# Differential attention with the two maps subtracted undivided, and the first map's sum folded into the head norm

## The chip, the cores and the metric

The kernel runs on one core of a Trainium2 chip. The metric is the device time of one execution in microseconds, as a median over runs. The core has five engines that matter here: TensorE (PE in the profile, with its weight loads as PEld), VectorE (DVE), ScalarE (ACT), GpSimd (POOL) and SyncE (SP), which issues most DMAs. Each engine works through its own queue in order, and they wait for each other by semaphores. In the views used below, times are microseconds from the start of the span unless marked ns, and L497 means line 497 of the kernel.

## The reference

The program is a decoder trunk of two layers over 512 tokens of width 1024. Each layer has a mixer (differential attention, a short convolution and a gated linear attention, whose outputs are concatenated and projected) and then a layer of 16384 single-neuron experts. The change touches the differential attention only:

```python
s = jnp.einsum('bqhmd,bkhmd->bhmqk', qi, k).astype(jnp.float32) * scale
p = jax.nn.softmax(jnp.where(mask, s, -jnp.inf), axis=-1)
a = p[:, :, 0] - lam * p[:, :, 1]
return jnp.einsum('bhqk,bkhe->bqhe', a.astype(v.dtype), v)
...
o = rmsnorm(o, gain) * out_scale
```

There are four heads, each with two maps (m = 0 and 1) of 64-wide queries and keys, and with values 128 wide. Each map has its own softmax. The second map is weighted with `lam`, one number per layer, and subtracted from the first; the difference is multiplied with the values. The result of each head is then normalised over its 128 columns (`rmsnorm`: divided by the root of the mean of its squares plus 1e-6). `lam` is exp(sum of lam_q1 * lam_k1) - exp(sum of lam_q2 * lam_k2) + lam_init.

## The kernel before, in words

The kernel runs the two layers one after the other, each as a mixer and an expert stage. The expert stages take most of the span and aren't touched. The mixer holds tokens in four blocks of 128 (`tb`). It projects the normalised input with slabs of 256 columns of the input weights; each product is three f32r matmuls of split operands (`mm3`, L79 to L81). `across` and `down` are generators that yield one projected tile (`psp`) at a time.

Attention runs for one block of queries at a time, in `diff_attention`, for tb = 0 to 3, with tb + 1 blocks of keys (128, 256, 384 or 512 columns). For each of the four heads:

- `head_weights` makes, for each map, one score product into PSUM (`pss`, L486), adds the causal mask by a second product (L487), and takes the row maximum (L488). The exponential (L493) reads PSUM, writes the map into the tile `e`, and gives the row's sum through its accumulator output, into a column of the small tile `st`. Then VectorE takes the reciprocal of both sums (L495), multiplies the second by `lam` (L496), scales the second map by it (L497), and scales the first map and subtracts the second in one instruction (L498).
- `diff_attention` transposes the difference on TensorE (`atr`, L512), copies it to SBUF (`aT`, L514, ScalarE), and multiplies it with the values into one quarter of the PSUM tile `po` (L516).

When all four heads of a block are in `po`, `head_norm` squares the whole tile (L524, ScalarE, 512 columns), sums the squares per head (L525, VectorE), makes the reciprocal root with a few small VectorE steps (`rsqrt`, L173 to L188) and scales `po` by it into `ho` (L527). `head_out` transposes that (`htr`, L535) and splits it for the output projection (`mh`, `ml`, L536 and L537).

The first two blocks are computed between the projections for the convolution (L375 to L382). The first two heads of block 2 are computed early, inside the last such projection (L393 to L396), and given to `diff_attention` as `early`. Blocks 2 and 3 run beside the loading and splitting of the output weights (`woraw` to `woh` and `wol`, L409 and L410) and beside the output projection (`pso`, L426), whose products with the other mixers' outputs don't need the attention.

The order of the instructions in each queue isn't that of the program text. A planner orders them from the data they need, the buffers that are free, the order in the text and the estimated cost of each, unless the text pins them (`keep_in_program_order`); nothing around this change in the mixer is pinned. So projection matmuls stand between those of the attention in TensorE's queue. PSUM holds four buffers for score tiles (`psA`), two for `po`, `atr` and `htr` (`psB`) and two for projections (`psC`). The small tiles `st` rotate through four buffers.

Of the kernel before, what the change touches and what calls it, by code (L numbers as in the profile page):

```python
# [7 lines left out]
F32 = mybir.dt.float32  # L8
# [5 lines left out]
AF = mybir.ActivationFunctionType  # L14
OP = mybir.AluOpType
AX = mybir.AxisListType
# [3 lines left out]
P = 128  # L20
# [43 lines left out]
def bc(ap, pattern):  # L64
    return bass.AP(tensor=ap.tensor, offset=ap.offset, ap=[ap.ap[0]] + pattern)


class K:
# [152 lines left out]
    def mixer(self, L):  # L221
        nc, tc, ins = self.nc, self.tc, self.ins
        lam_init = 0.8 - 0.6 * math.exp(-0.3 * L)
        right = ExitStack()
        with ExitStack() as mc:
# [4 lines left out]
            kT = mp.tile([P, 4, T], F32, name="kT")  # L230
# [7 lines left out]
            with ExitStack() as wc:  # L238
# [29 lines left out]
                def across(c0, n=256):  # L268
                    wh, wl = slab(c0, n)
                    for j in range(n // P):  # L270
                        ps = self.psC.tile([P, T], F32, tag="c", name="psp")
                        for k in range(KD):
                            self.mm3(ps, wh[:, k, j * P:j * P + P], wl[:, k, j * P:j * P + P], hh[:, k], hl[:, k],
                                     k == 0, k == KD - 1)
                        yield j, ps
# [34 lines left out]
                for i in range(2):  # L310
                    nc.vector.scalar_tensor_tensor(lt, lamv[:, 2 * i], 1.0, lamv[:, 2 * i + 1], op0=OP.mult,
                                                   op1=OP.mult, accum_out=ld[:, i:i + 1])
                le = mp.tile([P, 2], F32, name="le")
                nc.scalar.activation(le, ld, AF.Exp)
                lam = mp.tile([P, 1], F32, name="lam")
                nc.vector.tensor_tensor(lam, le[:, 0:1], le[:, 1:2], op=OP.subtract)
                nc.vector.tensor_scalar(lam, lam, lam_init, None, op0=OP.add)
                nc.vector.tensor_scalar(dgain, dgain, 1.0 - lam_init, None, op0=OP.mult)
                wh, wl = slab(2816, 272)
                for tb in range(TB):  # L320
# [25 lines left out]
                for i in range(4):  # L346
                    dst, h = (qT, kT)[i // 2], i % 2
# [18 lines left out]
                ap = ac.enter_context(tc.tile_pool(name="attn", bufs=2, side="right", reuse_waits="tile"))  # L366
                qz = [ap.tile([P, 4, 2, P], F32, name=f"qz{i}", bufs=1) for i in range(2)]
# [18 lines left out]
                for j in range(2):  # L386
                    y = yt[:, j]
                    nc.vector.tensor_scalar(y, z[:, j, 0:T], cw[:, j, 0:1], None, op0=OP.mult)
                    for w in (1, 2):
                        nc.vector.scalar_tensor_tensor(y, z[:, j, w:w + T], cw[:, j, w:w + 1], y,  # L390
                                                       op0=OP.mult, op1=OP.add)
                    ys.append(y)
                for j, ps in across(1536):  # L393
                    if j == 0:
                        self.turned_queries(2, qT, qz[0])
                        early = [self.head_weights(2, h, kT, qz[0], lam, ap) for h in range(2)]  # L396
                    nc.vector.tensor_tensor(ys[j], ys[j], ps, op=OP.mult)
                    self.split(mch[:, j], mcl[:, j], ys[j])

# [76 lines left out]
            r = slice(64 * m, 64 * m + 64)  # L476
            self.nc.scalar.copy(qz[r, :, m], qT[r, :, s])

    def head_weights(self, tb, h, kT, qz, lam, ap):
        nc = self.nc  # L480
        nk = (tb + 1) * P
        st = self.sm.tile([P, 8], F32, tag="st", name="st")
        pss = []
        for m in range(2):
            ps = self.psA.tile([P, T], F32, tag="a", name="pss")
            nc.tensor.matmul(ps[:, 0:nk], qz[:, h, m], kT[:, h, 0:nk], start=True, stop=False)  # L486
            nc.tensor.matmul(ps[:, tb * P:nk], self.identb, self.causal, start=False, stop=True)  # L487
            nc.vector.tensor_reduce(st[:, m:m + 1], ps[:, 0:nk], axis=AX.X, op=OP.max)  # L488
            pss.append(ps)
        nc.vector.tensor_scalar(st[:, 2:4], st[:, 0:2], -0.125, None, op0=OP.mult)  # L490
        e = ap.tile([P, 2, T], F32, tag="e", name="e")
        for m in range(2):
            nc.scalar.activation(e[:, m, 0:nk], pss[m][:, 0:nk], AF.Exp, bias=st[:, 2 + m:3 + m],  # L493
                                 scale=0.125, accum_out=st[:, 4 + m:5 + m])
        nc.vector.reciprocal(st[:, 6:8], st[:, 4:6])  # L495
        nc.vector.tensor_tensor(st[:, 7:8], st[:, 7:8], lam, op=OP.mult)  # L496
        nc.vector.tensor_scalar(e[:, 1, 0:nk], e[:, 1, 0:nk], st[:, 7:8], None, op0=OP.mult)  # L497
        nc.vector.scalar_tensor_tensor(e[:, 0, 0:nk], e[:, 0, 0:nk], st[:, 6:7], e[:, 1, 0:nk],  # L498
                                       op0=OP.mult, op1=OP.subtract)
        return e  # L500

    def diff_attention(self, tb, qT, kT, va, qz, lam, ap, early=()):
        nc = self.nc
        early = list(early)
        if not early:
            self.turned_queries(tb, qT, qz)
        po = self.psB.tile([P, 4, P], F32, tag="b", name="po")
        for h in range(4):
            e = early.pop(0) if early else self.head_weights(tb, h, kT, qz, lam, ap)
            tr = self.psB.tile([P, 4, P], F32, tag="b", name="atr")  # L510
            for kb in range(tb + 1):
                nc.tensor.transpose(tr[:, kb], e[:, 0, kb * P:kb * P + P], self.ident)  # L512
            aT = ap.tile([P, 4, P], F32, tag="aT", name="aT")
            nc.scalar.copy(aT[:, 0:tb + 1], tr[:, 0:tb + 1])  # L514
            for kb in range(tb + 1):
                nc.tensor.matmul(po[:, h], aT[:, kb], va[:, kb, h * P:h * P + P],  # L516
                                 start=(kb == 0), stop=(kb == tb))
        return self.head_norm(po, 4, P, ap)

    def head_norm(self, po, nh, hd, pool):  # L520
        nc = self.nc
        o = pool.tile([P, nh, hd], F32, tag="ho", name="ho", bufs=2)
        ss = self.sm.tile([P, nh], F32, tag="hss", name="hss")
        nc.scalar.activation(o, po, AF.Square)  # L524
        nc.vector.tensor_reduce(ss, o, axis=AX.X, op=OP.add)  # L525
        rstd = self.rsqrt(ss, hd)
        nc.vector.tensor_tensor(o, po, bc(rstd, [[1, nh], [0, hd]]), op=OP.mult)  # L527
        return o.rearrange("p h d -> p (h d)")

# [752 lines left out]
```

## Time and profile before

| what | us |
|---|---|
| median of 3 runs | 2959.73 |
| the runs | 2958.84 to 2962.85 |
| the profiled execution, its own time | 2958.37 |
| span of the profiled execution, first to last instruction | 2956.6 |

The granted TensorE clock was 0.999 of full speed. The profile gives busy time per engine, the same per stretch of the span, the idle time of an engine together with what released it, groups of instructions by line and shape, and the chain of work that ended last, followed backwards through the releasers. The matmuls are pipelined and their ends are modelled, so a busy TensorE isn't one at its peak. The lines that matter are shown in the prediction, where they are used.

### The profile page before, as it was taken

How to read it: one execution, taken by the hardware profiler on the slowest of the kernel's cores; microseconds unless marked ns; L12 is line 12 of the kernel's file. 1: busy time of each engine (PE TensorE's matmuls, PEld its weight loads, DVE VectorE, ACT ScalarE, POOL GpSimd, SP SyncE). 2: the span in 40 equal slices, each digit the busy share in tenths (PEclk: the TensorE clock that was granted, in tenths of full speed). 3: DMA queues.
4: the chain of work that ended last, by engine and by line, in shares of the span. 5: the costliest groups of instructions: out<-in, count | busy, mean ns of one | idle time of the engine just before them, and what ended most of it. 6: DMA issues, size and time to landing. Idle time of an engine off the chain costs nothing.

```text
span 2956.6 us, 44538 instructions
## 1 busy us (share of the span) xinstructions
PE 2925.6 (99%) x16262; PEld 2606.0 (88%) x16262; DVE 2394.7 (81%) x4754; ACT 1256.3 (42%) x1860; POOL 716.0 (24%) x617
## 2 busy tenths in 40 slices
PE   8999999999999999999999999999999999999998
PEld 7878899999999999888888788999999999988887
DVE  6676999976887788877866769999768787888778
ACT  6253355665333332333453433556653333333333
POOL 1200000222444455222012000012225444452220
PEclk9999999999999999999999999999999999999999
DMA  4322257999999998999633222679999999989995
GB/s 130 92 72 77 93 172 250 321 301 362 348 338 326 330 346 310 368 333 342 251 96 90 67 82 86 205 253 330 303 351 356 333 337 332 332 316 358 346 347 203
DMA packets 335835, 760.24 MB, mean 257 GB/s; under 512 B 30688, under 2 KB 191360, under 8 KB 331520
## 3 DMA queue, kind: packets, MB, share of 16 engines
q1 hardware_dynamic: 160624, 435.19, 41.4%
q0 software_dynamic: 75776, 271.62, 26.0%
q10 hardware_dynamic: 99216, 50.60, 5.7%
q8 instruction: 127, 2.08, 0.3%
q14 instruction: 92, 0.75, 0.1%
HBM read 673.15 MB, written 81.00 MB: 255 GB/s over the span
## 4 chain that ended last, share of the span: by engine, by line
PE 84%; DVE 11%; ACT 2%; issue 2%; DMA 1%; SPq 0%; DVEq 0%; ACTq 0%
PE pv L80 11%; PE pv L81 11%; PE pv L79 11%; PE psh L79 9%; PE psh L81 9%; PE psh L80 9%; PE psp L80 2%; PE psp L81 2%; PE psp L79 2%; PE psq L80 2%; PE psq L79 2%; PE psq L81 2%; PE pss L486 1%; PE psg L1211 1%; PE pss L764 1%
## 5 line engine op out<-in xcount | busy, mean ns | idle before, releaser
L827 POOL DMA_INDIRECT row<-in_u_rows,idx x256 | 349.1, 1363 | 1337.6 <-DVE row L834 627.8
L80 PE MATMUL pv<-vl,wh 128*128 128x512 f32 x1500 | 583.9, 389 | 0.4 <-DVE vl L931 0.3
L81 PE MATMUL pv<-vh,wl 128*128 128x512 f32 x1500 | 583.4, 389 | 0.0
L79 PE MATMUL pv<-vh,wh 128*128 128x512 f32 x1500 | 583.2, 389 | 0.0
L827 POOL DMA_INDIRECT row<-in_v_rows,idx x256 | 315.7, 1233 | 597.0 <-DVE yacc L843 548.2
L745 ACT ACTIVATE ht<-psh 128x384 f32<-128x384 f32 x256 | 125.7, 491 | 742.1 <-PE psh L81 741.9
L931 DVE TENSOR_TENSOR vl<-vraw,vh 128x1024 fp32r<-128x1024 f32 x250 | 305.9, 1224 | 115.2 <-ACT vh L936 104.2
L79 PE MATMUL psh<-ahi,uwb 128*128 128x384 f32 x1024 | 346.9, 339 | 0.0
L79 PE MATMUL psh<-ahi,uwa 128*128 128x384 f32 x1024 | 346.4, 338 | 0.0
L81 PE MATMUL psh<-ahi,uwa 128*128 128x384 f32 x1024 | 344.6, 337 | 0.7 <-DVE uwa L730 0.7
L80 PE MATMUL psh<-alo,uwa 128*128 128x384 f32 x1024 | 344.3, 336 | 0.0
L80 PE MATMUL psh<-alo,uwb 128*128 128x384 f32 x1024 | 344.2, 336 | 0.0
L81 PE MATMUL psh<-ahi,uwb 128*128 128x384 f32 x1024 | 344.1, 336 | 0.0
L81 PEld LDWEIGHTS pv<-vh,wl 128*128 128x128 f32 x1500 | 281.4, 188 | 59.6 <-DVE wl L931 1.0
L80 PEld LDWEIGHTS pv<-vl,wh 128*128 128x128 f32 x1500 | 281.4, 188 | 56.6 <-DVE vl L931 2.2
L79 PEld LDWEIGHTS pv<-vh,wh 128*128 128x128 f32 x1500 | 281.6, 188 | 53.9
L843 DVE SCALAR_TENSOR_TENSOR yacc<-row,wk,yacc 128x1024 f32<-128x1024 f32 x254 | 325.2, 1280 | 1.7
L944 ACT CAST wh<-ht 128x384 fp32r<-128x384 f32 x250 | 127.9, 512 | 433.6 <-DVE ht L1096 417.0
L834 DVE SCALAR_TENSOR_TENSOR row<-row,xg 128x1024 f32<-128x1024 f32 x256 | 308.0, 1219 | 0.0
L730 DVE TENSOR_TENSOR uwa<-uraw,uwa 128x1024 fp32r<-128x1024 f32 x144 | 175.7, 1223 | 134.7 <-ACT uwa L729 134.5
L936 ACT CAST vh<-vraw 128x1024 fp32r<-128x1024 f32 x250 | 262.6, 1050 | 9.7 <-DMA vraw<-in_v_rows 9.7
L730 DVE TENSOR_TENSOR uwb<-uraw,uwb 128x1024 fp32r<-128x1024 f32 x144 | 175.8, 1222 | 105.9 <-ACT uwb L729 105.9
(361 smaller groups left out, 5708.6 us busy)
## 6 DMA issues: line engine op xcount, KB each, us to landing
uraw<-in_peer_u SPq DMA_DIRECT2D x256, 512.0 KB, 5.6
vraw<-in_v_rows SPq DMA_DIRECT2D x256, 512.0 KB, 6.5
G<-stg ACTq DMA_DIRECT2D x48, 1024.0 KB, 7.6
g<-G SPq DMA_DIRECT2D x32, 1536.0 KB, 10.0
H<-ht SPq DMA_DIRECT2D x144, 192.0 KB, 4.7
ht<-H SPq DMA_DIRECT2D x144, 192.0 KB, 6.5
wraw<-in_w_in SPq DMA_DIRECT2D x84, 256.0 KB, 3.2
uraw<-in_peer_w_q SPq DMA_DIRECT2D x32, 512.0 KB, 3.5
```

The lines of the kernel that those rows point to most:

```text
L79: mm(ps, ah, bh, start=first, stop=False)
L80: mm(ps, ah, bl, start=False, stop=False)
L81: mm(ps, al, bh, start=False, stop=last)
L486: nc.tensor.matmul(ps[:, 0:nk], qz[:, h, m], kT[:, h, 0:nk], start=True, stop=False)
L730: self.last = pin(nc.vector.tensor_tensor(lo, src, hi.bitcast(F32), op=OP.subtract))
L745: pin(nc.scalar.activation(hs[c], ps, AF.Gelu))
L827: nc.gpsimd.indirect_dma_start(out=r, out_offset=None, in_=ins[name], in_offset=bass.IndirectOffsetOnAxis(ap=idx[:, k:k + 1], axis=0))
L834: nc.vector.scalar_tensor_tensor(r, r, 1.0, xg, op0=OP.mult, op1=OP.mult, accum_out=hd[:, k:k + 1])
L843: nc.vector.scalar_tensor_tensor(yacc, r, wk[:, k:k + 1], yacc, op0=OP.mult, op1=OP.add)
L931: self.last = pin(nc.vector.tensor_tensor(lo, src, hi.bitcast(F32), op=OP.subtract))
L936: pin(nc.scalar.copy(vh[c], vs[c]))
L944: pin(nc.scalar.copy(wh[c], hs[c]))
```

## The change

The division of each map by its sum is rewritten. With sums s0 and s1 of the exponentials e0 and e1, the difference e0/s0 - lam * e1/s1 is 1/s0 times (e0 - lam * s0/s1 * e1). The kernel now forms the bracket, with one VectorE instruction over the map, and multiplies it with the values undivided. The factor 1/s0 belongs to a row and a head, so it is applied behind the product: the four sums s0 of a block are collected in a tile `s0` of four columns, `head_norm` takes their reciprocal, passes it as scale to a Square per head (with the sum of squares through its accumulator output, in place of the reduce), and multiplies it into the norm's factor. `lam` is computed with its sign turned, so that the subtraction becomes an addition.

```diff
-                nc.vector.tensor_tensor(lam, le[:, 0:1], le[:, 1:2], op=OP.subtract)
-                nc.vector.tensor_scalar(lam, lam, lam_init, None, op0=OP.add)
+                nc.vector.tensor_tensor(lam, le[:, 1:2], le[:, 0:1], op=OP.subtract)
+                nc.vector.tensor_scalar(lam, lam, lam_init, None, op0=OP.subtract)
...
-                        early = [self.head_weights(2, h, kT, qz[0], lam, ap) for h in range(2)]
+                        s0 = self.sums()
+                        early = [s0] + [self.head_weights(2, h, kT, qz[0], lam, ap, s0) for h in range(2)]
...
-    def head_weights(self, tb, h, kT, qz, lam, ap):
+    def head_weights(self, tb, h, kT, qz, lam, ap, s0):
...
-        st = self.sm.tile([P, 8], F32, tag="st", name="st")
+        st = self.sm.tile([P, 6], F32, tag="st", name="st")
...
             nc.scalar.activation(e[:, m, 0:nk], pss[m][:, 0:nk], AF.Exp, bias=st[:, 2 + m:3 + m],
-                                 scale=0.125, accum_out=st[:, 4 + m:5 + m])
-        nc.vector.reciprocal(st[:, 6:8], st[:, 4:6])
-        nc.vector.tensor_tensor(st[:, 7:8], st[:, 7:8], lam, op=OP.mult)
-        nc.vector.tensor_scalar(e[:, 1, 0:nk], e[:, 1, 0:nk], st[:, 7:8], None, op0=OP.mult)
-        nc.vector.scalar_tensor_tensor(e[:, 0, 0:nk], e[:, 0, 0:nk], st[:, 6:7], e[:, 1, 0:nk],
-                                       op0=OP.mult, op1=OP.subtract)
+                                 scale=0.125, accum_out=st[:, 4:5] if m else s0[:, h:h + 1])
+        nc.vector.reciprocal(st[:, 4:5], st[:, 4:5])
+        nc.vector.scalar_tensor_tensor(st[:, 5:6], st[:, 4:5], lam, s0[:, h:h + 1], op0=OP.mult, op1=OP.mult)
+        nc.vector.scalar_tensor_tensor(e[:, 0, 0:nk], e[:, 1, 0:nk], st[:, 5:6], e[:, 0, 0:nk],
+                                       op0=OP.mult, op1=OP.add)
...
             self.turned_queries(tb, qT, qz)
+            s0 = self.sums()
+        else:
+            s0 = early.pop(0)
...
-        return self.head_norm(po, 4, P, ap)
-
-    def head_norm(self, po, nh, hd, pool):
+        return self.head_norm(po, 4, P, ap, s0)
+
+    def sums(self):
+        return self.sm.tile([P, 4], F32, tag="s0", name="s0")
+
+    def head_norm(self, po, nh, hd, pool, s0):
...
-        nc.scalar.activation(o, po, AF.Square)
-        nc.vector.tensor_reduce(ss, o, axis=AX.X, op=OP.add)
+        nc.vector.reciprocal(s0, s0)
+        for h in range(nh):
+            nc.scalar.activation(o[:, h], po[:, h], AF.Square, scale=s0[:, h:h + 1], accum_out=ss[:, h:h + 1])
         rstd = self.rsqrt(ss, hd)
+        nc.vector.tensor_tensor(rstd, rstd, s0, op=OP.mult)
         nc.vector.tensor_tensor(o, po, bc(rstd, [[1, nh], [0, hd]]), op=OP.mult)
```

More of the change, by code (lines that the diff above doesn't have):

```diff
@@ L506, in diff_attention @@
             self.turned_queries(tb, qT, qz)
+            s0 = self.sums()
+        else:
+            s0 = early.pop(0)
         po = self.psB.tile([P, 4, P], F32, tag="b", name="po")
         for h in range(4):
-            e = early.pop(0) if early else self.head_weights(tb, h, kT, qz, lam, ap)
+            e = early.pop(0) if early else self.head_weights(tb, h, kT, qz, lam, ap, s0)
             tr = self.psB.tile([P, 4, P], F32, tag="b", name="atr")
```

## The prediction

> **What bounds the kernel now.** I read the page first, its busy times and its chain, to learn which engine sets the end.
>
> ```profile
> PE 2925.6 (99%) x16262; PEld 2606.0 (88%) x16262; DVE 2394.7 (81%) x4754; ACT 1256.3 (42%) x1860; POOL 716.0 (24%) x617
> PE 84%; DVE 11%; ACT 2%; issue 2%; DMA 1%; SPq 0%; DVEq 0%; ACTq 0%
> ```
>
> TensorE is busy 99% of the span. The chain lies on VectorE for 11%, though, so I asked for the stretches in which the changed lines run: attention in layer 0 (150 to 250 us), attention in layer 1 (about 1619 to 1719 us), and for comparison the projections before them. The columns are the stretch, its length, then busy time with the instruction count of PE, PEld (weight loads), DVE, ACT and POOL, the granted clock, DMA share and GB/s.
>
> ```profile
> 100.00:150.00 50.00, 50.00 (x343) 46.28 (x342) 28.62 (x47) 14.83 (x27) 13.14 (x23) 1.00 0.33 85
> 150.00:200.00 50.00, 49.86 (x248) 37.35 (x247) 36.12 (x114) 23.56 (x69) 0.00 (x0) 1.00 0.15 48
> 200.00:250.00 50.00, 48.93 (x251) 35.99 (x250) 39.49 (x96) 25.58 (x51) 0.00 (x0) 1.00 0.31 106
> 1669.00:1719.00 50.00, 48.53 (x249) 36.53 (x250) 38.83 (x95) 26.15 (x52) 0.00 (x0) 1.00 0.32 106
> 1670.00:1690.00 20.00, 19.77 (x92) 13.20 (x91) 19.02 (x46) 12.95 (x25) 0.00 (x0) 1.00 0.50 155
> ```
>
> PE is busy there too, since the order of the work puts projection matmuls between the attention's own. VectorE is nearly full only in 1670 to 1690 us (19.02 of 20). Busy PE need not be PE at its peak, so I went to the waits, of the matmuls over the whole run, then of the weight loads in the two attentions (total us, times, longest):
>
> ```profile
> PE po L516 <- ACT aT L514: 1.2, 2, 0.6
> ...
> PE pso L79 <- ACT woh L84: 0.9, 2, 0.6
> ```
> ```profile
> PEld po L516 <- ACT aT L514: 5.4, 16, 0.9
> ...
> PEld atr L512 <- issue: 1.1, 4, 0.4
> ...
> PEld htr L535 <- DVE ho L527: 0.5, 1, 0.5
> PEld pso L80 <- DVE wol L85: 0.4, 2, 0.2
> ...
> PEld pso L80 <- DVE st L490: 0.3, 1, 0.3
> ```
> ```profile
> PEld po L516 <- ACT aT L514: 5.0, 15, 0.9
> PEld pso L79 <- ACT woh L84: 1.7, 2, 1.1
> ...
> PEld htr L535 <- DVE ho L527: 0.5, 1, 0.5
> ```
>
> The result of the edited head chain is `e`, written at L498 and read by the transposes `atr` at L512. No row names L498 as releaser: the transposes wait 1.1 us in all, for their own issue. So the instruction which the change brings forward has nobody waiting for it.
>
> **The change part by part.** These are the groups by line, shapes kept apart (busy us, mean ns):
>
> ```profile
> L525 DVE TENSOR_REDUCE hss<-ho 128x4 f32<-128x512 f32 x8 | 5.5, 684 | 12.5 <-ACT ho L524 12.5
> L495 DVE RECIPROCAL st<-st 128x2 f32<-128x2 f32 x32 | 5.2, 163 | 7.3 <-ACT e L493 7.3
> L496 DVE TENSOR_TENSOR st<-st,lam 128x1 f32<-128x1 f32 x32 | 5.0, 157 | 0.7
> ...
> L497 DVE TENSOR_SCALAR e<-e,st 128x512 f32<-128x512 f32 x8 | 3.9, 483 | 0.3
> L497 DVE TENSOR_SCALAR e<-e,st 128x384 f32<-128x384 f32 x8 | 3.3, 418 | 0.4
> L185 DVE SCALAR_TENSOR_TENSOR rt<-rt 128x1 f32<-128x1 f32 x20 | 3.2, 159 | 0.6
> L497 DVE TENSOR_SCALAR e<-e,st 128x256 f32<-128x256 f32 x8 | 2.8, 350 | 0.4
> ...
> L497 DVE TENSOR_SCALAR e<-e,st 128x128 f32<-128x128 f32 x8 | 2.3, 282 | 0.4
> ```
>
> *Each of 32 heads.* The scaling of the second map (L497) goes: 8 x (0.282 + 0.350 + 0.418 + 0.483) = 12.3 us of VectorE. The reciprocal stays, one column instead of two. The one-column multiply by lam (0.157) becomes a one-column scalar_tensor_tensor, for which L185 is the nearest row (0.159): nothing. The subtraction L498 keeps its form and sizes. Writing the first map's sum into another tile costs nothing, and the two lines for lam only swap operands.
>
> *Each of 8 blocks.* The reduce goes: 8 x 0.684 = 5.5 us. A reciprocal and a multiply on four columns come in: 8 x (0.163 + 0.157) = 2.6 us. VectorE is left 12.3 + 5.5 - 2.6 = 15.2 us lighter. One Square of 512 columns becomes four of 128, each with an accumulator read. The trace has no such Square; the nearest rows are the exponentials of 128 columns, which have a pointer operand and an accumulator too (start, us), and beside them the last block's end in layer 0:
>
> ```profile
> 153.10 0.36 ACT L493 ACTIVATE e<-pss,st 128x128 f32<-128x128 f32 x1
> ...
> 154.14 0.37 ACT L493 ACTIVATE e<-pss,st 128x128 f32<-128x128 f32 x1
> 154.39 0.21 ACT L493 ACTIVATION_READ_ACCUMULATOR e<-pss,st 128x1 f32 x1
> ```
> ```profile
> 233.91 0.60 ACT L524 ACTIVATE ho<-po 128x512 f32<-128x512 f32 x1 [1.25 <-PE po L516]
> 238.56 0.69 ACT L536 ACTIVATE mh<-htr,dgain 128x512 fp32r<-128x512 f32 x1 [4.05 <-PE htr L535]
> ```
> ```profile
> 235.26 0.17 DVE L173 TENSOR_SCALAR rv<-hss 128x4 f32<-128x4 f32 x1
> 235.46 0.17 DVE L175 TENSOR_SCALAR ry<-rv 128x4 int32<-128x4 int32 x1
> ```
>
> Four such exponentials in a row take from 153.10 to 154.39 + 0.21 = 154.60: 1.50 us. In the place of the Square's 0.60, ScalarE gets 0.90 more per block, 7.2 us in all, and has room for it on the whole (42%). From Square to the first step of the norm it was 235.26 - 233.91 = 1.35 us and becomes 1.50: 0.15 longer. The extra multiply adds one step of the small operations, 235.46 - 235.26 = 0.20. The reciprocal of the sums needs only the last head's exponential and the sums' last reader, so it is done while that head is transposed and multiplied. Each block's end is 0.35 us longer. This is taken from the exponentials, since they do the same work in form; the other end is four Squares as cheap as the one, 0.60, with one read behind it (154.39 + 0.21 - 154.14 - 0.37 = 0.09): then the end would be 1.35 - 0.69 - 0.20 = 0.46 shorter.
>
> [...]
>
> *What lies on the path.* First, the end of block 3, once per layer: `htr` waits for `ho` (0.5 us in both lists), so 0.35 more is exposed, 0.7 in all. Output projection matmuls that don't need this block stand right behind, and the order written for the longer chain can put one of them ahead: I take half, +0.4; without that cover it is 0.7, and with cheap Squares the waits of 0.5 go.
>
> Second, the output weights. In layer 1 their split (L84, L85) shares VectorE's full stretch, 1670 to 1690 us, with four of the L497, whose row for that stretch is
>
> ```profile
> 1670.00:1690.00 20.00, 1.79 (x4) 1.00 0.50 155
> ```
>
> and with block 2's reduce: 1.79 + 0.68 = 2.5 us go, and 0.3 come back. Raw buffers come free sooner by up to that much, so the last load is issued sooner, and the 0.9 us for which PE waited for `woh` can go: -0.9. The bounds are nothing, and all that weight loads waited for `woh`, `ho` (twice), `wol` and `st`: 1.7 + 0.5 + 0.5 + 0.4 + 0.3 = 3.4 us. What is late next is PE itself, which has no long wait here besides that for `aT`.
>
> Third, the other heads and the ends of blocks 0 to 2: 0, since nobody waits for L498, and no wait of `htr` is listed but the one. The waits for `aT` (L514) are those of transpose, copy and product in turn, which the change leaves alone. No DMA, no matmul, no POOL instruction is added or moved past another.
>
> The sum: 0.4 - 0.9 + 0 = -0.5 us. Made against the profiled execution it is 2958.37 - 0.5 = 2957.9 us (span 2956.6 and 1.8 around it). The median of the three runs lies 1.36 us above that execution, so the median to expect is 2959.73 - 0.5 = 2959.2 us. A measurement of this kernel tells about 0.2% from no change, 5.9 us; the forecast is no difference.
>
> **The rivals.** *The head chain paces attention.* If PE's filling only hides that attention runs at the pace of VectorE, each head gives back its L497: 12.3 us, so 2959.7 - 12.3 = 2947.4. For it speaks the weight loads' share, 37.35 and 35.99 of 50 us against 46.28 in the projections. Against it: the weight loads' waits for VectorE come to 0.5 + 0.4 + 0.3 = 1.2 us in the first list, none for L498. [...] The lower share has another source, though: a score product holds PE longer per weight load than a projection of the same width,
>
> ```profile
> L80 PE MATMUL psp<-alo,wh 128*128 128x512 f32 x48 | 19.4, 405 | 0.0
> ...
> L486 PE MATMUL pss<-kT,qz 128*128 128x512 f32 x16 | 8.2, 607 | 0.0
> ```
>
> 607 against 405 ns, which is no wait. Chance 0.05.
>
> *ScalarE's queue at the blocks' ends becomes the wait* (the other side). The four Squares stand in ScalarE's order ahead of the next copy of `aT`, for which PE already waits most. If each block hands its 0.90 us to PE, and block 3's ends stay bare, that is 7.2 + 0.7 = 7.9 us, 2967.6. It decides where a transposed head is ready within 0.9 us behind a Square, with no projection matmul to run. For it: 5.4 and 5.0 us of such waits. Against it: behind the last block ScalarE is idle for 4.05 us, and matmuls pass the waits of the copies nearly unhurt (1.2 us over the run). If one block per layer pays, it is 1.8 us, within 0.2%. Chance 0.05.
>
> *The order moves.* The order is planned from estimated costs, so shorter VectorE steps can shuffle matmuls, loads and buffers beyond the edited lines. The two layers give a measure: from block 0's third score product to the last block's `ho` the chain has
>
> ```profile
> 151.77 0.28 PE pss L486 x2
> ```
> ```profile
> 237.12 0.70 DVE ho L527
> ```
> ```profile
> 1619.42 0.28 PE pss L486 x2
> ```
> ```profile
> 1705.13 0.70 DVE ho L527
> ```
>
> that is 85.35 us in layer 0 and 85.71 in layer 1, with different neighbours: 0.36 apart. To pass 5.9 us, some sixteen such differences would have to add up. Half of that is 2959.7 plus or minus 3; all of it 2953.8 or 2965.6. Chance 0.08: half stays within 0.2%, a quarter lies on each side.
>
> **How the numbers follow.** The forecast has 0.82. Faster by over 0.2%: 0.05 + 0.02 = 0.07. Slower: 0.05 + 0.02 = 0.07. Within: 0.82 + 0.04 = 0.86. The range takes the forecast's bounds, 2959.7 - 3.4 = 2956.3 and 2959.7 + 0.7 + 1.8 (one block per layer pays on ScalarE) = 2962.2, and about a microsecond more on either side for the median of runs that lie from 2958.84 to 2962.85: 2955.0 to 2963.0.
>
> **What would show it.** Right: VectorE's busy time near 2379.5 us, ScalarE's near 1263.5, PE's within 2 us; no L497; four Squares from first start to last read about 1.5 us; the wait of `htr` for `ho` 0.5 to 0.9; the wait for `woh` under 0.9. Wrong: attention's 85 us shorter or longer by over 2 us; a row of waits that names the new Squares or `aT` with several us more; or unlike stretches outside attention.

## The result, and the profile after

The changed kernel takes 2981.14 us (median of 6 runs, 2979.63 to 2983.89) against 2959.31 for the one before (6 runs beside them, 2957.44 to 2963.61). The ratio is 1.0072, 95% interval 1.0061 to 1.0083: slower by some 22 us, where no difference was forecast. The profiled execution took 2980.36 us, with a span of 2978.6.

The page of the changed kernel, busy times and chain:

```profile
PE 2950.5 (99%) x16262; PEld 2627.7 (88%) x16262; DVE 2382.4 (80%) x4730; ACT 1260.0 (42%) x1916; POOL 710.5 (24%) x617
PE 92%; DVE 3%; DMA 2%; ACT 2%; issue 1%; SPq 0%; ACTq 0%; DVEq 0%
```

VectorE is lighter, as forecast. TensorE is 24.9 us busier with the same 16262 matmuls, and the chain lies on it more than before. So the matmuls themselves got dearer. Which ones, the starts of the first and the last of a kind tell (us, lengths from the exact starts; `psh` is the experts' key product, `pv` the product with their values):

| stretch | before | after | longer by |
|---|---|---|---|
| start to first `psh`, layer 0 (mixer, queries) | 375.1 | 374.7 | -0.4 |
| first `psh` to last `pv`, layer 0 | 375.1 to 1485.2 | 374.7 to 1495.8 | 11.1 |
| last `pv` to first `psh` of layer 1 (mixer, queries) | 357.6 | 358.2 | 0.6 |
| first `psh` to last `pv`, layer 1 | 1842.8 to 2948.3 | 1854.1 to 2970.1 | 10.6 |

The loss stands in the two expert stages, which the change doesn't touch. The stretch from 375 to 1466 us, of the kernel before and then of the changed one (columns as in the prediction), says what kind of loss it is:

```profile
375.00:1466.00 1091.00, 1089.69 (x6095) 995.92 (x6094) 914.44 (x1416) 472.78 (x634) 331.90 (x256) 1.00 0.89 318
```
```profile
375.00:1466.00 1091.00, 1089.36 (x6045) 995.98 (x6044) 902.89 (x1399) 466.17 (x626) 330.07 (x256) 1.00 0.90 317
```

TensorE is busy all the time in both, at the full clock (1.00) and beside the same DMA traffic (318 and 317 GB/s), but it gets through 50 fewer matmuls. Its idle time in this stretch is 1.3 us before and 1.6 after, so no wait of any size has come in; each matmul takes a little longer. The instructions on `psh`, before and after (duration in ns as least, median and most; first and last start in us):

```profile
L79 PE MATMUL psh<-ahi,uwa x1024: 332/336/423, 375.1 to 2620.8; 128*128 128x384 f32 x171
```
```profile
L79 PE MATMUL psh<-ahi,uwa x1024: 336/338/422, 374.7 to 2642.4; 128*128 128x384 f32 x171
```

Matmul ends are modelled, so the starts are the better measure. In both layers a group of 24 `psh` and one of 18 `pv` often follow each other in turn. Here are the first matmuls of successive groups, before and after:

```profile
902.75 0.34 PE L79 MATMUL psh<-ahi,uwb 128*128 128x384 f32 x1
906.92 0.39 PE L79 MATMUL pv<-vh,wh 128*128 128x512 f32 x1
911.00 0.34 PE L79 MATMUL psh<-ahi,uwa 128*128 128x384 f32 x1
```
```profile
901.69 0.34 PE L79 MATMUL psh<-ahi,uwb 128*128 128x384 f32 x1
905.93 0.40 PE L79 MATMUL pv<-vh,wh 128*128 128x512 f32 x1
910.05 0.34 PE L79 MATMUL psh<-ahi,uwb 128*128 128x384 f32 x1
```

A `psh` group takes 4.17 us before (173.5 ns from one start to the next) and 4.24 after (176.7); a `pv` group 4.08 and 4.12. From the exact starts, a pair takes 8.247 us before and 8.360 after (medians of 102 pairs in each kernel, 51 to a layer). Within a `psh` group the steps were 173 ns behind a first of 178; now they run about 180, 175, 178, 174 over and over. In a `pv` group only the start is slow: 233, 236, 224, 231, 236, 228, 232, 231 ns, then 227 as before. Together the terms make the loss: 102 pairs by 0.113 us are 11.5, the steps of the other 3696 `psh` sum to 9.4 us more, and `pv` waits 1.7 us longer for its split operands `vl` and `vh` (2.0 in place of 0.3). That is 22.6 in all against 22.0 in the span.

**The two theories.** What the diff does hand to the expert stages is room in SBUF. Tiles lie one behind another, and the new tile `s0` has four buffers that take 32 B each. So every tile that the build places behind the small pool moves up by 128 B per partition, among them all that the experts stream, while the split activations `ahi` and `alo`, placed ahead of it, stay. In the build, `uwa` (the weights of `psh`) goes from 80544 to 80672, and `wh` and `vh` (weights and moving operand of `pv`) from 200864 and 205472 to 200992 and 205600; `ahi` (the moving operand of `psh`) is at 34688 in both. The theory of the *places* (A in the expectations below) says that this shift slows the matmuls. Its rival, the theory of the *order* (B), says that the planner, given other costs and one more tile to hold, wrote an order that feeds TensorE worse, or that the change itself costs something which shows up late.

### The profile page after: what moved, and what is told of

It reads as the page before. It is cut to its first block, busy times and chain, and to the rows that moved or that the text cites. A ratio compares the mean times of both kernels' runs of the same rounds, so it can differ in the third digit from the quotient of the medians.

```text
span 2978.6 us, 44588 instructions
## 1 busy us (share of the span) xinstructions
PE 2950.5 (99%) x16262; PEld 2627.7 (88%) x16262; DVE 2382.4 (80%) x4730; ACT 1260.0 (42%) x1916; POOL 710.5 (24%) x617
## 4 chain that ended last, share of the span: by engine, by line
PE 92%; DVE 3%; DMA 2%; ACT 2%; issue 1%; SPq 0%; ACTq 0%; DVEq 0%
PE psh L79 12%; PE psh L80 12%; PE psh L81 12%; PE pv L80 11%; PE pv L79 11%; PE pv L81 11%; PE psp L80 2%; PE psp L79 2%; PE psp L81 2%; PE psq L80 2%; PE psq L79 2%; PE psq L81 2%; PE psg L1219 1%; PE psg L1220 1%; PE pss L772 1%
## 5 line engine op out<-in xcount | busy, mean ns | idle before, releaser
L835 POOL DMA_INDIRECT row<-in_v_rows,idx x256 | 308.0, 1203 | 610.9 <-DVE yacc L851 561.4
L738 DVE TENSOR_TENSOR uwb<-uraw,uwb 128x1024 fp32r<-128x1024 f32 x144 | 175.8, 1221 | 107.5 <-ACT uwb L737 107.3
```

The lines of the kernel that those rows point to most:

```text
L738: self.last = pin(nc.vector.tensor_tensor(lo, src, hi.bitcast(F32), op=OP.subtract))
L835: nc.gpsimd.indirect_dma_start(out=r, out_offset=None, in_=ins[name], in_offset=bass.IndirectOffsetOnAxis(ap=idx[:, k:k + 1], axis=0))
```

## The experiments

**1. The kernel before, with 128 B more in the small pool.** All four buffers of `st` are widened; the order of the instructions in every queue is that of before.

```diff
-        st = self.sm.tile([P, 8], F32, tag="st", name="st")
+        st = self.sm.tile([P, 16], F32, tag="st", name="st")
```

> The kernel before, every instruction in the same place of its queue; only the small tile st is declared with 16 columns where 8 are used, so that all that lies behind the small pool is 128 bytes per partition higher, as it is in the changed kernel. Theory A (the addresses): the hidden products psh of the expert stages go from a mean of 336 to 338 ns and from a step of 173.5 to about 176.7 ns, and the kernel takes 2978 to 2983 us, as the changed one does. Theory B (the new order of the instructions): psh stays at 336 ns, 2957 to 2962 us.

Measured: 2985.12 us (2984.6 to 2986.19), ratio 1.008 [1.0063, 1.0096]. Its `psh`:

```profile
L79 PE MATMUL psh<-ahi,uwa x1024: 334/338/423, 378.2 to 2646.8; 128*128 128x384 f32 x171
```

Nothing is computed differently, and the loss is there whole: a pair of groups takes 8.360 us, as in the changed kernel, and the two expert stages take 1121.1 and 1115.9 us (1121.1 and 1116.0 there). The places suffice. The time lies 2 us above the expected range and 4 above the changed kernel; in the profiles that is the mixers with the queries, 737.6 us in sum against 732.9.

**2. The change without a new tile.** The four sums go into spare columns of `hss`, whose buffers take 32 B anyway. Nothing moves behind the small pool.

```diff
-        return self.sm.tile([P, 4], F32, tag="s0", name="s0")
+        return self.sm.tile([P, 8], F32, tag="hss", name="hss")
...
-        ss = self.sm.tile([P, nh], F32, tag="hss", name="hss")
+        ss, s0 = s0[:, nh:2 * nh], s0[:, 0:nh]
```

> The changed kernel, whole, but the four sums s0 lie in the unused half of the padded tile hss, so that no tile behind the small pool moves against the kernel before. Theory A (the addresses): psh back at 336 ns, and the time is what the change itself is worth, 2957 to 2961 us (mixer 0.5 us shorter or so). Theory B (the order): psh at 338 ns, 2978 to 2983 us.

Measured: 2960.9 us (2955.39 to 2963.22, 10 runs), ratio 0.9997 [0.9987, 1.0007]. This is what the change costs by itself: nothing that can be measured, as the prediction had it. Its first line and its wait at the block's end:

```profile
PE 2924.6 (99%) x16262; PEld 2606.9 (88%) x16262; DVE 2382.1 (81%) x4730; ACT 1263.5 (43%) x1916; POOL 715.8 (24%) x617
```
```profile
PE htr L543 <- DVE ho L535: 0.4, 2, 0.2
```

**3. Only a part moved.** The widened tile is `xg`, which is placed behind the stream of `uwa`. So `uwa` stays, and the values' stream (`wh`, `vh`) moves.

```diff
-            xg = pp.tile([P, D], F32, name="xg")
+            xg = pp.tile([P, D + 32], F32, name="xg")[:, 0:D]
```

> The kernel before, with xg declared 32 columns wider: in the expert stages all that is allocated behind xg (gathered rows, v rows, gate tiles, yacc) is 128 bytes higher, while the tiles of the hidden products (uraw, uwa, uwb, ht) stay; the instructions are the same. Theory A, if it is the addresses of the weights in uwa and uwb: psh at 336 ns, about 2960 us. Theory A, if it is the tiles that others write or DMAs fill at the same time: psh slower, 2970 us or more. Theory B: 2957 to 2962 us.

Measured: 2970.1 us (2967.55 to 2972.51), ratio 1.003 [1.0019, 1.0041]. Part of the loss, and neither reading under theory A fits whole: the time is that of the second, but `psh` keeps its median of 336 ns, as in the first. The first matmuls of successive groups:

```profile
896.72 0.34 PE L79 MATMUL psh<-ahi,uwb 128*128 128x384 f32 x1
900.90 0.39 PE L79 MATMUL pv<-vh,wh 128*128 128x512 f32 x1
905.03 0.34 PE L79 MATMUL psh<-ahi,uwb 128*128 128x384 f32 x1
```

Now both groups are slow at their start alone: the first seven `psh` take 174 to 178 ns and the first nine `pv` 224 to 236, and then each runs at its old 173 and 227. A pair takes 8.307 us, which makes 6.1 of the 9 us over 102 pairs; `pv` waits 2.0 us longer for `vl` and `vh`. So there are two effects: one on the steady pace of a group (in `psh` 176.7 ns in place of 173.5 in the changed kernel), and one that lasts some eight matmuls at each switch.

**4. Moved by 256 B.** `st` is widened to 24 columns (e1 in the expectation is experiment 1).

```diff
-        st = self.sm.tile([P, 8], F32, tag="st", name="st")
+        st = self.sm.tile([P, 24], F32, tag="st", name="st")
```

> As e1, with 24 columns: all behind the small pool is 256 bytes higher; the instructions are the same. Theory A with a conflict that depends on the address modulo 256: as the kernel before, 2957 to 2962 us. Theory A with a longer period or with the distance to the unmoved inputs: slower, 2965 us or more. Theory B: 2957 to 2962 us.

Measured: 2958.89 us (2957.6 to 2961.1), ratio 0.999 [0.998, 1.0001], with `psh` back at 336 ns:

```profile
L79 PE MATMUL psh<-ahi,uwa x1024: 332/336/423, 375.1 to 2621.1; 128*128 128x384 f32 x171
```

So 128 B cost the whole loss and 256 B nothing, as with a period of 256 B. With a shorter power of two, 128 B would have cost nothing either.

**5 and 6. Relation or place.** In the first, the constants ahead of `ahi` and `alo` are widened by 128 B, so that these move with the rest and keep their distance to it; in the second, `st` takes 128 B more besides, so that the streams stand where they did, modulo 256, and `ahi` and `alo` don't.

```diff
-        self.rs3 = cp.tile([P, 1], F32, name="rs3")
+        self.rs3 = cp.tile([P, 40], F32, name="rs3")[:, 0:1]
```
```diff
-        st = self.sm.tile([P, 8], F32, tag="st", name="st")
+        st = self.sm.tile([P, 16], F32, tag="st", name="st")
```

> The kernel before, with its first constant 160 B wide instead of 4: now the constants behind it, the activations ahi and alo, and every tile that the small pool pushes stand 128 B higher; x alone and the tiles of the right side (attention's, the gates') stand where they stood. The instructions and their order are those of before. Known: the rest 128 B higher with ahi and alo unmoved costs 24 us, all 256 B higher costs nothing. Theory 'relation' (the pace of a matmul hangs on how its weights lie to its moving operand, modulo 256 B): psh has its two operands as they lay to each other before, so 336 ns and steps of 173.5 ns, and a time within 4 us of 2961. Theory 'place' (it hangs on where the weights themselves begin): uwa and uwb begin where they do in the slow kernels, so 338 ns, steps of 176.7 ns and some 2983 us.

> The kernel before, with its first constant 160 B wide and st 64 B: ahi and alo stand 128 B higher, the tiles that the small pool pushes 256 B, so the weights of the experts begin where they did modulo 256 B and the moving activations do not. Same instructions in the same order. Theory 'relation': the two are as far apart as in the slow kernels, so psh 338 ns, steps of 176.7 ns, and some 2980 us. Theory 'place of the weights': as before, 336 ns and within 4 us of 2961. Should both this and the run with all of them 128 B higher be slow, the place of each of the two counts by itself.

Measured: 2962.54 us (2961.32 to 2965.83), ratio 1.0003 [0.9992, 1.0015], and 2980.68 us (2980.32 to 2986.03), ratio 1.0073 [1.0049, 1.0097]. Their `psh`, in this order:

```profile
L79 PE MATMUL psh<-ahi,uwa x1024: 332/336/423, 373.7 to 2626.4; 128*128 128x384 f32 x171
```
```profile
L79 PE MATMUL psh<-ahi,uwa x1024: 337/338/422, 375.9 to 2643.0; 128*128 128x384 f32 x171
```

The relation decides. The weights of `psh` at their slow place are fast when the moving operand has moved along, and at their fast place slow when it has moved away. In both fast layouts the weights lie 32 B above the moving operand, modulo 256; in the slow ones 160.

**7. TensorE alone.** Groups of 24 matmuls with the moving operand and the weights each at eight places 32 B apart (`STEPS` holds them as columns of 4 B); no other engine works beside them (ScalarE is busy for 10.4 us with the operands, for which the first matmul waits 17.8, and VectorE for 0.7 of the 653.8 us of the span).

```python
for n in (384, 512):
    for mo in STEPS:
        for wo in STEPS:
            t = ps.tile([P, n], F32, tag="t", name=f"n{n}m{4 * mo}w{4 * wo}x")
            for k in range(KD):
                h = mov[:, mo + 512 * k:mo + 512 * k + n]
                l = mov[:, 4096 + mo + 512 * k:4096 + mo + 512 * k + n]
                wh = wts[:, wo + 128 * k:wo + 128 * k + 128]
                wl = wts[:, 1024 + wo + 128 * k:1024 + wo + 128 * k + 128]
                nc.tensor.matmul(t, wh, h, start=(k == 0), stop=False)
                nc.tensor.matmul(t, wh, l, start=False, stop=False)
                nc.tensor.matmul(t, wl, h, start=False, stop=(k == KD - 1))
```

> TensorE alone: groups of 24 matmuls (three by eight, as the experts' splits), 384 and 512 columns wide, with the moving operand and the weights begun at each of 8 x 8 places 32 B apart; the model's computation is left out whole, so the output is not the reference's and its whole time is of no interest. The moving tile begins at 32896 and the weights at 66176, both 128 over a multiple of 256. If the place of the operands in SBUF alone sets the pace, the mean step of a group differs between the places with a period of 256 B: some 173.5 ns against 176.7 ns at 384 columns, along the diagonals of the table (by the relation) or its columns (by the place of the weights) or rows (by that of the moving). If the pace needs another engine or a DMA beside it (a meeting of two users of one place), all 64 groups of a width keep one step within 0.5 ns.

Measured: the step follows the distance, not either place. The mean step of the second half of a group in ns, as a median over the eight pairs of places with the same distance (weights less moving operand, modulo 256 B):

| distance, B | 0 | 32 | 64 | 96 | 128 | 160 | 192 | 224 |
|---|---|---|---|---|---|---|---|---|
| 384 columns | 173.3 | 173.7 | 174.6 | 173.4 | 175.8 | 176.6 | 173.9 | 176.4 |
| 512 columns | 227.3 | 233.1 | 233.4 | 233.6 | 233.5 | 233.6 | 228.8 | 232.7 |

But for three cells at 384 columns, the eight agree within 0.3 ns at 384 and 1 ns at 512. One of the three is the first group of the run, which begins with steps of 320 ns; the other two are 3 ns off (176.4 at distance 96, 172.9 at 224), as much as the effect itself, and that isn't explained. The kernel before stands at distance 32 for `psh` and 0 for `pv`, and whole groups there step by 173.5 and 227.0 ns in this run, as in the kernel (173.5 and 227); the changed kernel stands at 160 for `psh`, with 176.6 here and 176.7 there. The trace has it in the first matmuls of successive groups (the name tells columns, place of the moving operand and place of the weights):

```profile
489.56 0.39 PE L46 MATMUL n512m128w128x<-mov,wts 128*128 128x512 f32 x1
495.01 0.39 PE L46 MATMUL n512m128w160x<-mov,wts 128*128 128x512 f32 x1
500.60 0.40 PE L46 MATMUL n512m128w192x<-mov,wts 128*128 128x512 f32 x1
```

24 matmuls of 512 columns take 5.45 us at distance 0 and 5.59 at distance 32. With no other engine at work, the pace follows from how the two operands lie to each other. What makes it so inside isn't shown.

**8. TensorE alone, two kinds in turn.** The groups are like `psh` and `pv`, with u the distance within `psh` and v the distance of both operands of `pv` from the moving operand of `psh`. `group` takes a name, the columns, the number of steps of three matmuls, and the places of the moving operand and of the weights.

```python
for u in (8, 0, 40):
    for v in STEPS:
        for r in range(6):
            group(f"u{4 * u}v{4 * v}hx", 384, 8, 0, u)
            t = group(f"u{4 * u}v{4 * v}vx", 512, 6, v, v)
```

> TensorE alone again, the model's computation left out whole: six times in turn a group like psh (24 matmuls of 384 columns, weights u bytes from the moving operand) and one like pv (18 of 512 columns, weights and moving operand both v bytes from psh's moving operand), for u of 32, 0 and 160 and v of 0 to 224. The kernel before has u 32 and v 32, the changed one 160 and 160, the run with the value stage alone moved 32 and 160, the one with chosen places 0 and 0. If the slow matmuls at the start of a group come of TensorE's own rhythm, u32v32 starts pv at 227 ns at once, u160v160 and u32v160 take some eight matmuls of 231 to 236 ns, u0v0 as many in pv and six of 175 to 185 ns in psh. If another engine's work at the switch makes them, all groups start as evenly as u32v32.

Measured: the pairs of all four layouts come out to the nanosecond (medians of six pairs each). The place of the kernel before, then that of the changed one:

```profile
78.23 0.34 PE L44 MATMUL u32v32hx<-mov,wts 128*128 128x384 f32 x1
82.39 0.39 PE L44 MATMUL u32v32vx<-mov,wts 128*128 128x512 f32 x1
86.47 0.34 PE L44 MATMUL u32v32hx<-mov,wts 128*128 128x384 f32 x1
```
```profile
1073.86 0.34 PE L44 MATMUL u160v160hx<-mov,wts 128*128 128x384 f32 x1
1078.11 0.40 PE L44 MATMUL u160v160vx<-mov,wts 128*128 128x512 f32 x1
1082.22 0.34 PE L44 MATMUL u160v160hx<-mov,wts 128*128 128x384 f32 x1
```

| layout | TensorE alone, us a pair | in the kernel, us a pair |
|---|---|---|
| u 32, v 32 (before) | 8.247 | 8.247 |
| u 160, v 160 (the change) | 8.360 | 8.360 |
| u 32, v 160 (experiment 3) | 8.307 | 8.307 |
| u 0, v 0 (experiment 9) | 8.307 | 8.307 |

The slow starts are there too: at u 160, v 160 the steps of the `pv` group begin 233, 236, 224, 231, 236, 228, 233, 230 and settle at 227. So they come in a program that has no work for another engine beside the matmuls, as does the steady pace: after a switch a group falls into its rhythm at once (the `pv` of the kernel before: 228 ns, then 227) or after some eight matmuls, depending on the places. The layout of before is the best of the 24 tried, with 8.247 us a pair.

**9. Places chosen by the table.** The change of experiment 2, with tiles widened so that the wide matmuls have distance 0, where the first table is best.

```diff
-                mcl = mo.tile([P, 2, T], F32R, name="mcl")
+                mcl = mo.tile([P, 2 * T + 24], F32R, name="mcl")[:, 0:2 * T].rearrange("p (k t) -> p k t", k=2)
...
-                lam = mp.tile([P, 1], F32, name="lam")
+                lam = mp.tile([P, 32], F32, name="lam")[:, 0:1]
...
-        o = pool.tile([P, nh, hd], F32, tag="ho", name="ho", bufs=2)
+        o = pool.tile([P, nh * hd + 24], F32, tag="ho", name="ho", bufs=2)[:, 0:nh * hd].rearrange("p (h d) -> p h d", h=nh)
...
-                s2 = self.sm.tile([P, 2], F32, tag="s2", name="s2", bufs=1)
+                s2 = self.sums()[:, 0:2]
```

> The change with its sums in hss, and the tiles placed so that the widest matmuls have weights and moving operand at one place modulo 256 B: everything behind the small pool 32 B lower (the last norm's s2 goes into hss), so uwa and uwb begin where ahi and alo do, lam widened by 96 B and mcl by 96 B, so the mixers' weights do as well, and ho by 2 x 96 B, so the attention's tiles keep their place to the mix tiles. The table of TensorE alone gives 227.3 ns for 512 columns there against 233.1 (query maps, now 32 B apart), 228.8 (the first mixer maps, 192 apart) and 233.6 (half of the output maps, 160 apart), and 173.3 against 173.7 ns for psh. In the profile before, the steps of the query maps lie 3.3 us over 227.3 ns in sum, the first mixer maps' 1.3, the output maps' 1.3, and 6144 psh at 0.3 ns give 1.8: theory 'relation' expects 4 to 8 us less than before, 2953 to 2957 us. If the relation counted in the experts alone, or the gain were eaten at the switches from one kind of group to the next, 2959 to 2963 us.

Measured: 2967.42 us (2962.55 to 2970.8, 11 runs), ratio 1.0015 [1.0006, 1.0024]. This forecast was wrong: the time lies outside both of its ranges. Its steady part held: the median step of the query maps went from 232 to 227 ns, that of the output maps from 232 to 227, and from the first query product to the first `psh` it takes 105.1 us in each layer against 106.1 in experiment 2. But `psh` and `pv` now start slowly at each switch:

```profile
896.52 0.33 PE L79 MATMUL psh<-ahi,uwb 128*128 128x384 f32 x1
900.71 0.39 PE L79 MATMUL pv<-vh,wh 128*128 128x512 f32 x1
904.83 0.33 PE L79 MATMUL psh<-ahi,uwb 128*128 128x384 f32 x1
```

102 pairs by 0.060 us are 6.1 us back. The waits of `pv` for `vh` and `vl` are 3.6 us against 0.8 in experiment 2, but they lie between 0.3 and 4.9 us in the other runs, so that part isn't shown to come from the places. The second half of the forecast's last sentence, the gain eaten at the switches, is what happened, with more than the gain. Experiment 8, made afterwards, shows the same 8.307.

**10. The changed kernel with 128 B more.** No instruction differs from the changed kernel.

```diff
-        return self.sm.tile([P, 4], F32, tag="s0", name="s0")
+        return self.sm.tile([P, 16], F32, tag="s0", name="s0")[:, 0:4]
```

> The changed kernel with nothing edited but the width of its new tile: 64 B for each of the four buffers of s0 instead of 16 (which take 32), so everything behind the small pool stands 256 B above its place in the kernel before instead of 128. No instruction is added, taken away or moved. Theory 'relation': psh 336 ns in steps of 173.5 ns, and the time of the change proper, 2957 to 2963 us. The rival, that the new order or the longer life of the sums costs the 22 us, keeps 2980 us and 338 ns.

Measured: 2958.27 us (2954.84 to 2963.65, 10 runs), ratio 0.9997 [0.9987, 1.0006]. The whole loss is gone by widening the tile that brought it.

```profile
PE 2925.2 (99%) x16262; PEld 2606.5 (88%) x16262; DVE 2382.0 (81%) x4730; ACT 1262.8 (43%) x1916; POOL 715.6 (24%) x617
```

No version beat the kernel before by more than can be measured.

## Why the prediction was wrong, and where it was right

**The step that failed** is the sentence "Writing the first map's sum into another tile costs nothing". It priced the instruction, rightly, and not the tile. The tile's 128 B moved the experts' streams against the activations, and the step of 6144 `psh` went from 173.5 to 176.7 ns and the start of the `pv` groups with it: 22 us, shown by experiment 1 (the shift without the change) and experiments 2 and 10 (the change without the shift). None of the rivals had it. The rival of the planner's order came nearest, since it looked beyond the edited lines, but the order is shown to be innocent: the same order as in the changed kernel takes 2958.27 us in experiment 10. Its last words, "unlike stretches outside attention", named the sign by which it would be wrong, and that is where the trace showed it.

**The change proper** came out as forecast: 2960.9 and 2958.27 us without the shift, against 2959.2 forecast. Its terms, from the changed kernel's trace. The last block's end in layer 0, first on ScalarE, then on VectorE:

```profile
231.85 0.37 ACT L532 ACTIVATE ho<-po,s 128x128 f32<-128x128 f32 x1 [1.25 <-PE po L519]
...
232.21 0.36 ACT L532 ACTIVATE ho<-po,s 128x128 f32<-128x128 f32 x1
...
233.15 0.21 ACT L532 ACTIVATION_READ_ACCUMULATOR ho<-po,s 128x1 f32 x1
```
```profile
233.39 0.17 DVE L173 TENSOR_SCALAR rv<-hss 128x4 f32<-128x4 f32 x1 [2.50 <-ACT ho L532]
...
235.38 0.69 DVE L535 TENSOR_TENSOR ho<-po,ry 128x512 f32<-128x512 f32 x1
```

- Four Squares take 233.15 + 0.21 - 231.85 = 1.51 us, forecast 1.50. The exponentials were the right row to take. Without the last read the trace has 1.42, a Square beginning every 0.35 us.
- From the first Square to `ho` it is 235.38 - 231.85 = 3.53 us, before 237.12 - 233.91 = 3.21: longer by 0.32, forecast 0.35.
- ScalarE's busy time is 7.2 us more in experiment 2 and 6.5 in experiment 10, forecast 7.2. In the changed kernel itself it is only 3.7 more. Experiments 1 and 6, the kernel before with the same distance of 160, have 2.6 and 2.5 us less than the kernel before, so the difference goes with the places; how isn't shown.

VectorE was to be 15.2 us lighter and is 12.3 (2394.7 to 2382.4). The rows of the changed lines:

```profile
L497 DVE SCALAR_TENSOR_TENSOR st<-st,lam,s 128x1 f32<-128x1 f32 x32 | 6.9, 216 | 0.6
...
L530 DVE RECIPROCAL s<-s 128x4 f32<-128x4 f32 x8 | 1.4, 171 | 0.0
...
L534 DVE TENSOR_TENSOR ry<-ry,s 128x4 f32<-128x4 f32 x8 | 1.3, 162 | 0.3
```

The mis-sized term is L497, where L185 (0.159) was taken as the nearest row: it takes 216 ns against the 157 of the multiply that it replaces, 1.9 us over 32 heads. The nearer row was L179, whose scalar is a column of a tile as well and not a constant, 220 ns. That leaves 13.3, and the last microsecond lies elsewhere.

The waits of the matmuls, too, are those forecast:

```profile
PE po L519 <- ACT aT L517: 1.2, 2, 0.6
...
PE htr L543 <- DVE ho L535: 0.5, 2, 0.3
```

The wait for `woh` is gone, `htr` waits 0.5 us (forecast 0.5 to 0.9), `aT` is unchanged, and no wait names the Squares. Both rivals on the edited chain fall with experiments 2 and 10.

One more sign of being wrong was met, though it hardly moved the time. The prediction gave the other heads 0, said that no matmul is moved past another, and would have called itself wrong if attention changed by over 2 us. From the first score product to the last `ho` it was 86.35 and 86.71 us in the two layers and is 84.21 and 84.11. The order did move: of the 192 output projection matmuls of a layer, 58 stood ahead of the last `po` before and 51 stand there now. Seven by some 0.23 us are 1.6 us of other work that was moved behind, and from the last `po` to the first query product it takes 36.9 us in both layers where it took 35.2. So most of the gain on the chain is work put off. What is left, from the first score product to the first query product, is 118.0 to 117.2 us in layer 0 and 118.4 to 117.2 in layer 1, and experiments 2 and 10 show it too (117.0 to 117.2). The two microseconds are too few for the times of whole runs to show.

The changed kernel's own table hides them, because the shift cost the mixers something as well. From the first projection of layer 0 to its first score product it takes 119.2 us in the kernel before and in experiments 2 to 5 and 10, and 120.6 to 120.7 in the three layouts with distance 160 (the changed kernel, experiments 1 and 6). The way from layer 0's last `pv` to the first score product of layer 1 is 133.1 to 133.6 us in the former and 134.6 to 134.9 in the latter. In the build the wide projections stand at distance 64 there and at 192 in the kernel before, 233.4 against 228.8 ns in the table of experiment 7.

## What to carry to other kernels

A change that adds, drops or resizes an SBUF tile can move every tile placed behind it, as it did here, where the move cost 22 us on a kernel whose TensorE is busy for 99% of the span, and the change itself nothing that can be measured: look at the starts of matmuls that weren't edited before explaining a difference by the lines that were. To tell the two apart, pad the old kernel by the bytes that the new one adds, and pad the new one until the shift is a multiple of 256 B, the period found here. Where a layout is to be chosen, time the groups in the turn in which they run, since the best pace of each by itself (experiment 9) wasn't the best together: 8.307 us a pair against 8.247.

## What the runs showed of the hardware

The pace of matmuls back to back depends on the distance between their weights and their moving operand in SBUF, modulo 256 B: 173.3 to 176.6 ns at 384 columns and 227.3 to 233.6 at 512 (medians of eight pairs of places), with TensorE alone. After a switch between two kinds of matmuls the steps can be uneven for some eight matmuls (224 to 236 ns in place of 227), and whether they are depends on the places as well. Both were measured with f32r operands and 128 x 128 weights loaded for every matmul. Whether other types or reused weights show it, and what inside TensorE or SBUF makes the period of 256 B, wasn't tried.
